# Where the second modulation's rows are stored and fetched, and when the gate's sums are turned

## Chip, cores and metric

The kernel runs on one core of a Trainium2 chip. The metric is the device time of one execution in microseconds, as the median of several runs. The engines named are TensorE (PE, with its weight loads as PEld), VectorE (DVE), ScalarE (ACT), GpSimd (POOL) and SyncE (SP), whose queue issues nearly all DMA transfers here.

## The reference, cut to what matters

A two-layer decoder on 512 tokens of width 2048, in float32. Layer 0 is differential attention; from its output shared keys and values are made, and layer 1 is forgetting attention over them. Each layer has a modulation from a conditioning vector `c`: a shift, a scale and a gate.

```python
c_act = jax.nn.silu(c)
for l in range(DEPTH):
    mod = c_act @ w_mod[l] + b_mod[l]
    shift, scale, gate = jnp.split(mod, 3, axis=-1)
    h = x * (1.0 + scale[:, None]) + shift[:, None]
    if l < N_A:
        y = diff_attention(h, ...)
    else:
        if kv is None:
            kv = shared_kv(x, c_act, kv_w_mod, kv_b_mod, kv_w, kv_b_f)
        y = forgetting_attention(h, b_w_in[l - N_A], b_w_out[l - N_A], *kv)
    x = layer_norm(DN_ALPHA * x + gate[:, None] * y, ln_g[l], ln_b[l])
```

The change is about `mod` of layer 1. Its shift and scale are needed before the first query projection, `h @ w_q`; its gate only at the end.

## The kernel before

**Products.** Every large product is made of float32 numbers split in a high and a low part, so that three matmuls (lines 345 to 347) make one. Weights come as 512 KB steps into staging buffers (`wst`, four of them), ScalarE rounds them to the high part (`whi`, line 245), and VectorE takes the low part (`wlo`, line 246). `WeightStream` (line 176) does this ahead of use: `get` (line 274) sees to it that two further steps are split and up to three further ones loaded. Its loads pass through a hook, `ws.keep`, which is normally the identity.

**Runs, bursts and ticks.** A projection to 512 columns is one call of `group` (line 494), a *run*: 8 steps of two column blocks of the input, each step with four *bursts* of six matmuls, one burst for each of four accumulators. After every burst comes a *tick* (line 478): it takes one entry from the list `pieces` and calls what is in it, and then takes as many steps of the current `background` generator as the run's `bg` says for this tick. Ticks of a run are counted from 0 to 31. So `pieces` and `bg` say beside which burst other work is written down.

**What sets the order.** Outside the kernel's first stage a planner orders each engine's instructions. It goes by the order in which the program writes them down, by when it reckons that data and buffers are there, and so it may put a later instruction first where the earlier one would wait. `tc.keep_in_program_order(ins)` pins an instruction behind the one that was written down last for the same engine. A buffer that is taken again waits until the last use of its former content is over.

**The second modulation.** `w_mod[1]` is not multiplied on TensorE. VectorE scales each 128-row block by its entries of `c_act` and adds it to an accumulator (`macc`). `mod_stream` (line 545) does this for shift and scale, four times 1024 columns with 16 sums each, one sum to a step of the generator; then two steps *turn* the accumulator (transposition and reduction, lines 646 and 647). Five empty steps later a small product on TensorE (line 657) adds up the partial sums. Two additions (line 660) put the bias and the 1 on, and the rows are stored to `mod_dram` (line 661). The steps are spent in the two middle runs of layer 0's output projection (13 ticks each, line 1473), in the first key run (10, line 1947) and in the later key runs (`TICKS`, line 48: 16, 16, and the first nine of the last run).

`end_of_sums` (line 1567) takes all steps that are left. `fetch_rows(1)` (line 1581) reads the rows back in another layout, and `fold(1)` (line 1585) transposes them on TensorE (line 1588) and makes the columns `mod_a` and `mod_b`. From these `build_h` (line 1664) makes the operands of the query projections, 16 blocks of high and low parts, after the steps 3 to 7 of the last key run and directly behind it. It uses two buffers with the tag `htmp`.

**The gate.** The first 1024 columns of the gate begin in the last key run: `gate_start` (line 1489) makes six of 16 sums (`FORE`) with three load buffers (`ms`), and turns them with `turn_gate` (line 1483), also through `htmp`. The first query run goes on with the other ten, in `gate_stream` (line 1516): loads and accumulator are in the buffer `gs` (line 1978). Then come one step for each of two turns, two empty steps, and one step with the product (lines 1547 and 1548), an addition (line 1549) that writes into `gs`, and the store to `gate_dram` (line 1550). `gs` has the same tag as `pT` (line 1983), the turned probabilities of the forgetting attention, and there is one buffer with that tag.

**Query runs.** The runs over `bj[p]` (line 2171) project the queries and gates of two heads each. From `p = 1` on they carry the attention of the pair before in `pieces` (line 2130). Entry 6 of the first pair takes the buffer of `pT` and sends the first block of turned probabilities there (line 2078), entries 16 and 17 multiply by the values (line 2099).

Of the kernel before, what the change touches and what calls it, by code (L numbers as in the profile page):

```python
# [16 lines left out]
P = 128  # L17
D = 2048
KT = D // P
# [29 lines left out]
UNIT = 9  # L49
FORE = 6  # L50
# [3 lines left out]
class Job:  # L54
# [14 lines left out]
    def load(self, nc, dst, s, keep):  # L69
        rows = self.src[2 * s * P : (2 * s + 2) * P, :]  # L70
        off = 0
        for c, n in self.parts:
            keep(nc.sync.dma_start(dst[:, :, off : off + n], rows[:, c : c + n].rearrange("(k p) n -> p k n", p=P)))
            off += n
# [205 lines left out]
def tile_yoco(  # L280
# [23 lines left out]
    nc = tc.nc  # L304
# [19 lines left out]
    mod_dram = [dram.tile([2, D], F32, name=f"mod_dram{k}") for k in range(2)]  # L324
# [8 lines left out]
    def tr_bank(name="tr"):  # L333
        return ps.tile([P, 512], F32, name=name, tag="tr", bufs=1)
# [61 lines left out]
    rows = {}  # L396
# [42 lines left out]
    ws = WeightStream(nc, wpool)  # L439
# [12 lines left out]
    bj = [Job(b_w_in, [(256 * p, 256), (2048 + 256 * p, 256)]) for p in range(8)]  # L452
# [22 lines left out]
    pieces = []  # L475
# [65 lines left out]
    def cols(name):  # L541
        return const.tile([P, KT], F32, name=name)


    def mod_stream(segs, new_stage, new_acc, ahead):

        todo = [(i, kt) for i in range(len(segs)) for kt in range(KT)]
        loaded, turned_sums = [], []

        def load_upto(k):  # L550
            while len(loaded) < min(k + 1, len(todo)):
                i, kt = todo[len(loaded)]
                src, col, _ = segs[i]
                loaded.append(new_stage())
                nc.sync.dma_start(loaded[-1], src[kt * P : (kt + 1) * P, col : col + 1024])

        for k, (i, kt) in enumerate(todo):
            load_upto(min(k + ahead, max([k, *limit[-1:]])) if limit else k + ahead)
            w, one = loaded[k], cact[:, kt : kt + 1]
            loaded[k] = None  # L560
            if kt == 0:
                acc = new_acc()
                ins = V.tensor_scalar(acc, w, one, None, op0=ALU.mult)
            else:
                ins = V.scalar_tensor_tensor(acc, w, one, acc, op0=ALU.mult, op1=ALU.add)  # L565
            tc.keep_in_program_order(ins)
            if kt == 4:
                while turned_sums:
                    next(turned_sums.pop(0), None)
            yield  # L570
            if kt == KT - 1:
                for half, steps in enumerate(segs[i][2]):
                    turned_sums.append(steps(acc[:, 512 * half : 512 * half + 512]))
                    next(turned_sums[-1])
                    yield
        for _ in range(5):
            yield
        for steps in turned_sums:
            next(steps, None)
# [90 lines left out]
    with tc.tile_pool(name="start", bufs=2, reuse_waits="tile") as sp, tc.manual_schedule(engines=MANUAL):  # L670
# [4 lines left out]
        tiles = []  # L675
# [308 lines left out]
        at = [0] * 4  # L984
# [267 lines left out]
    def drain():  # L1252
        while pieces:
            tick(0)
# [9 lines left out]
    def keep(key, acc):  # L1264
        raw[key] = kpool.tile([P, T], F32, name="raw", tag="K")
        S.copy(raw[key], acc)
# [105 lines left out]
    def ktile(name):  # L1372
        return kpool.tile([P, T], F32, name=name, tag="K")
# [105 lines left out]
    ab, rows = {}, {}  # L1479
# [3 lines left out]
    def turn_gate(t, acc, red, f):  # L1483
        V.transpose(t, acc[:, 512 * f : 512 * f + 512])
        V.tensor_reduce(
            red[:, 16 * f : 16 * f + 16], t.rearrange("p (j q) -> p j q", q=32), axis=mybir.AxisListType.X, op=ALU.add
        )

    def gate_start(red, upto):

        tiles = []

        def load():
            tiles.append(npool.tile([P, 1056], F32, name="ms", tag="ms", bufs=3)[:, 0:1024])
            kt = len(tiles) - 1
            nc.sync.dma_start(tiles[kt], w_mod[1][kt * P : (kt + 1) * P, 2 * D : 2 * D + 1024])

        load()
        load()
        yield  # L1500
        acc = npool.tile([P, 2, 512], F32, name="macc", tag="macc", bufs=1).rearrange("p a b -> p (a b)")
        for kt in range(upto):
            if kt + 2 < upto:
                load()
            w, one = tiles[kt], cact[:, kt : kt + 1]
            if kt == 0:
                ins = V.tensor_scalar(acc, w, one, None, op0=ALU.mult)
            else:
                ins = V.scalar_tensor_tensor(acc, w, one, acc, op0=ALU.mult, op1=ALU.add)
            tc.keep_in_program_order(ins)  # L1510
            yield
        for f in range(2):
            turn_gate(npool.tile([P, 512], F32, name="mturn", tag="htmp", bufs=2), acc, red, f)
            yield
# [52 lines left out]
    def end_of_sums():  # L1567
        for _ in background:
            pass
# [8 lines left out]
        return fn  # L1578


    def fetch_rows(k):
        rows[k] = ktile("mrow")
        nc.sync.dma_start(rows[k][0 : 2 * KT, 0:P], mod_dram[k].rearrange("v (a p) -> (v a) p", p=P))

    def fold(k):
        row = rows[k]
        pt = tr_bank()
        PE.transpose(pt[:, 0 : 2 * KT], row[0 : 2 * KT, 0:P], ident[0 : 2 * KT, 0 : 2 * KT])
        a1, b1 = cols(f"mod_a{k}"), cols(f"mod_b{k}")
        V.tensor_tensor(b1, pt[:, KT : 2 * KT], bncol, op=ALU.mult)  # L1590
        V.tensor_tensor(b1, pt[:, 0:KT], b1, op=ALU.add)
        V.tensor_tensor(a1, pt[:, KT : 2 * KT], gcol, op=ALU.mult)
        return a1, b1
# [91 lines left out]
    def evac_k(g):  # L1685
        def fn(b, acc):
            KTs[4 * g + b] = ktile("kT")
            S.copy(KTs[4 * g + b], acc)
        return fn
# [11 lines left out]
    def back_k():  # L1701
        for b in range(TB):
            KTs[b] = ktile("kT")
            nc.sync.dma_start(KTs[b], k_dram[b])
# [208 lines left out]
    for i, (half, s) in enumerate(lag):  # L1913
# [14 lines left out]
        for b in (2 * half, 2 * half + 1):  # L1928
            bs = slice(b * P, (b + 1) * P)
            for kq in range(2):  # L1930
                kt = 2 * s + kq
# [24 lines left out]
    for g in range(1, 4):  # L1956
        if g == 3:
            back_k()
            early = gate_start(gate_first, FORE)
            plan = [None] * 3 + [partial(next, early, None)] * (FORE + 3)  # L1960
            plan += [None] * (UNIT + 7 - len(plan))
            for at, fn in ((UNIT, lambda: (end_of_sums(), fetch_rows(1))), (UNIT + 6, lambda: ab.update(b=fold(1)))):
                plan[at] = [plan[at], fn] if plan[at] else fn
            pieces.extend(plan)
        group(
            kj[g], False, evac_k(g), bg=lambda k, g=g: TICKS[g](k),
            after_sub=(lambda s: build_h(late.get(s, ()), ab.get("b"))) if g == 3 else None,
        )
# [18 lines left out]
    def evac_b(p):  # L1987
        def fn(b, acc):
            hd = 2 * p + b % 2
            if b < 2:  # L1990
                hi = bp.tile([P, T], F32R, name="qh", tag="qh", bufs=2)
                lo = bp.tile([P, T], F32R, name="ql", tag="ql", bufs=2)
                S.activation(hi, acc, AF.Copy, scale=QS)
                V.scalar_tensor_tensor(lo, acc, QS, hi.bitcast(F32), op0=ALU.mult, op1=ALU.subtract)
                cur[hd, "q"] = (hi, lo)
            else:
                th = bp.tile([P, T], F32, name="thb", tag="biasb", bufs=2)
                sg = bp.tile([P, T], F32, name="sgb", tag="sgb", bufs=2)
                S.activation(th, acc, AF.Tanh, scale=0.5)
                V.scalar_tensor_tensor(sg, th, 1.0, acc, op0=ALU.add, op1=ALU.mult)  # L2000
                cur[hd, "sgT"] = sg
        return fn
# [10 lines left out]
    def load_pair(p):  # L2013
        load_v(2 * p)
        for hd in (2 * p, 2 * p + 1):
            nf = bp.tile([P, T], F32, name="nfb", tag="nfb", bufs=2)
            row_bcast(nf, f_dram[hd, :])
            cur[hd, "nf"] = nf
# [131 lines left out]
    def split_ogb(hds):  # L2150
        for hd in hds:
            new_h(hd)
            split(Hh[hd], Hl[hd], ogB[hd])

    load_pair(0)
    for p in range(8):
        if p:
            pieces.extend(attention_pair(p - 1))

        def before(s, p=p):  # L2160
            if s == 7:
                drain()
                if p:
                    load_pair(p)
                split_pair(p)

        def after(s):
            if s >= 1:
                split_ogb((2 * s - 2, 2 * s - 1))

        group(
            bj[p], False, evac_b(p), bg=0 if p > 1 else (lambda k: k < 4 or k == 9) if p else (lambda k: k % 3 == 1),
            before_sub=before, after_sub=after if p == 7 else None,
        )

# [174 lines left out]
```

## Time and profile before

| | us |
|---|---|
| median of 3 runs | 1911.6 |
| lowest and highest run | 1910.22, 1914.89 |
| profiled execution | 1911.24 |
| its span, first to last instruction | 1909.4 |
| mean clock granted to TensorE | 0.999 of full |
| DMA transfers | 402.23 MB |

Times of single instructions below are microseconds from the start of the span. A row of the order in time gives the start, the duration, the engine, the line, the operation with its tiles, and in brackets how long the engine was idle before it and what ended that. TensorE starts a matmul every 0.23 us though a row shows some 0.39, since matmuls overlap. "SPq" rows are issues on SyncE's queue, with the time of issuing. Several issues that follow each other are merged in one row, with the waits between them.

### The profile page before, as it was taken

To read this page: it belongs to the slowest core of one execution; us is meant where nothing else is said; L and a number is where in the kernel's file an instruction comes from. 1 tells how busy PE (TensorE), PEld (TensorE's weight loads), DVE (VectorE), ACT (ScalarE), POOL (GpSimd) and SP (SyncE) were. 2 spreads that over 40 slices of the span, in tenths; PEclk is the share of its full clock that TensorE was granted. 3 is DMA by queue.
4 is the path that set the end of the run, shared out by engine and by line. 5 is a ranking of instruction groups with operands and counts; after the bars stand their busy time and mean duration, and the time that the engine had idled before them with its cause. 6 is when DMAs were issued, how large, how long until landed. Compare 5 with 4: busy or idle time off the path is not lost.

```text
span 1909.4 us, 25683 instructions
## 1 busy us (share of the span) xinstructions
PE 1893.7 (99%) x8829; PEld 1579.2 (83%) x8829; DVE 1433.2 (75%) x2685; ACT 778.6 (41%) x1328; POOL 2.3 (0%) x12
## 2 busy tenths in 40 slices
PE   8999999999999999999999999999999999999998
PEld 7888888888888888888888889887888888888887
DVE  8994588777777778667687877877766666687888
ACT  3656344323333344531275643226344434453122
POOL 0000000000000000000000000000000000000000
PEclk9999999999999999999999999999999999999999
DMA  9993566676767676476658679884655555555952
GB/s 349 385 338 92 155 191 198 213 231 194 235 192 239 190 236 182 133 251 229 189 187 276 211 211 305 304 294 150 203 157 154 151 156 153 160 171 160 323 168 111
DMA packets 350994, 402.23 MB, mean 211 GB/s; under 512 B 77144, under 2 KB 258548, under 8 KB 349584
## 3 DMA queue, kind: packets, MB, share of 16 engines
q1 hardware_dynamic: 347184, 395.20, 65.2%
q10 hardware_dynamic: 3680, 5.40, 0.8%
q8 instruction: 69, 1.13, 0.2%
q14 instruction: 61, 0.50, 0.1%
HBM read 363.46 MB, written 37.04 MB: 210 GB/s over the span
## 4 chain that ended last, share of the span: by engine, by line
PE 92%; DVE 3%; DMA 2%; SPq 1%; issue 1%; ACT 0%; DVEq 0%; ACTq 0%
PE acc L345 24%; PE acc L346 24%; PE acc L347 24%; PE acc L903 4%; PE sc L903 2%; PE sc L347 2%; PE sc L346 2%; PE sc L345 2%; PE o L347 1%; PE o L345 1%; PE o L346 1%; PE o L903 1%; DMA ms<-in_w_mod_dram 1%; SPq L751 1%; DVE wlo L246 0%
## 5 line engine op out<-in xcount | busy, mean ns | idle before, releaser
L245 ACT CAST whi<-wst 128x1024 fp32r<-128x1024 f32 (+2 forms) x294 | 305.4, 1039 | 558.5 <-PE acc L347 217.2
L246 DVE TENSOR_TENSOR wlo<-wst,whi 128x1024 fp32r<-128x1024 f32 (+2 forms) x294 | 354.6, 1206 | 202.4 <-ACT whi L245 192.5
L345 PE MATMUL acc<-hh,whi 128*128 128x512 f32 x1184 | 463.3, 391 | 0.0
L346 PE MATMUL acc<-hl,whi 128*128 128x512 f32 x1184 | 461.5, 390 | 0.0
L347 PE MATMUL acc<-hh,wlo 128*128 128x512 f32 x1184 | 460.6, 389 | 0.0
L345 PE MATMUL acc<-whi,hh 128*128 128x512 f32 (+1 forms) x912 | 353.5, 388 | 0.0
L346 PE MATMUL acc<-wlo,hh 128*128 128x512 f32 (+1 forms) x912 | 352.2, 386 | 0.0
L347 PE MATMUL acc<-whi,hl 128*128 128x512 f32 (+1 forms) x912 | 351.8, 386 | 0.0
L347 PEld LDWEIGHTS acc<-hh,wlo 128*128 128x128 f32 x1184 | 222.3, 188 | 47.3
L345 PEld LDWEIGHTS acc<-hh,whi 128*128 128x128 f32 x1184 | 222.4, 188 | 43.3 <-issue 0.9
L346 PEld LDWEIGHTS acc<-hl,whi 128*128 128x128 f32 x1184 | 222.6, 188 | 42.4
L347 PEld LDWEIGHTS acc<-whi,hl 128*128 128x128 f32 x912 | 171.2, 188 | 35.0 <-DVE hl L1624 0.2
L345 PEld LDWEIGHTS acc<-whi,hh 128*128 128x128 f32 x912 | 171.3, 188 | 32.9 <-ACT hh L1623 0.2
L346 PEld LDWEIGHTS acc<-wlo,hh 128*128 128x128 f32 x912 | 171.4, 188 | 32.4
L618 DVE SCALAR_TENSOR_TENSOR macc<-ms,cact,macc 128x512 f32<-128x512 f32 x180 | 133.7, 743 | 20.8 <-DMA ms<-in_kv_w_mod_dram 13.6
L801 DVE SCALAR_TENSOR_TENSOR sacc<-sms,cact,sacc 128x512 f32<-128x512 f32 (+1 forms) x128 | 89.9, 702 | 5.1 <-DMA sms<-in_w_mod_dram 1.6
L1097 ACT ACTIVATE e<-e,mn 128x128 f32<-128x128 f32 (+3 forms) x64 | 36.1, 563 | 112.1 <-DVE mn L1093 105.5
L565 DVE SCALAR_TENSOR_TENSOR macc<-ms,cact,macc 128x1024 f32<-128x1024 f32 x60 | 76.7, 1278 | 3.2 <-DMA ms<-in_w_mod_dram 2.6
L2057 ACT ACTIVATE eb<-eb,mnb 128x128 f32<-128x128 f32 (+1 forms) x64 | 36.0, 562 | 62.2 <-DVE mnb L2054 62.0
L903 PE MATMUL acc<-wlo,hh 128*128 128x512 f32 x128 | 50.0, 399 | 0.3 <-DVE wlo L265 0.3
L903 PE MATMUL acc<-whi,hl 128*128 128x512 f32 x128 | 49.4, 393 | 0.0
L903 PE MATMUL acc<-whi,hh 128*128 128x512 f32 x128 | 49.2, 393 | 0.0
(414 smaller groups left out, 2511.1 us busy)
## 6 DMA issues: line engine op xcount, KB each, us to landing
wst<-in_a_w_in_dram SPq DMA_DIRECT2D x240, 256.0 KB
ms<-in_w_mod_dram SPq DMA_DIRECT2D x102, 512.0 KB
ms<-in_kv_w_mod_dram SPq DMA_DIRECT2D x64, 512.0 KB
wst<-in_b_w_in_dram SPq DMA_DIRECT2D x128, 256.0 KB
wst<-in_kv_w_dram SPq DMA_DIRECT2D x59, 512.0 KB
sms<-in_w_mod_dram SPq DMA_DIRECT2D x56, 512.0 KB
wst<-in_a_w_out_dram SPq DMA_DIRECT2D x32, 512.0 KB
wst<-in_b_w_out_dram SPq DMA_DIRECT2D x32, 512.0 KB
```

Of the source, the lines that this page charges most:

```text
L245: self.nc.scalar.copy(hi, st)
L246: self.nc.vector.tensor_tensor(lo, st, hi.bitcast(F32), op=ALU.subtract)
L345: PE.matmul(dst, lhs[0], rhs[0], start=start, stop=False, skip_group_check=True)
L346: PE.matmul(dst, lhs[0], rhs[1], start=False, stop=False, skip_group_check=True)
L347: PE.matmul(dst, lhs[1], rhs[0], start=False, stop=stop, skip_group_check=True)
L565: ins = V.scalar_tensor_tensor(acc, w, one, acc, op0=ALU.mult, op1=ALU.add)
L618: ins = V.scalar_tensor_tensor(acc, w, cact[:, kt : kt + 1], acc, op0=ALU.mult, op1=ALU.add)
L751: (queue or nc.sync).dma_start(mtile[n][:, kq : kq + step, v, :], rows.rearrange("(k p) n -> p k n", p=P))
L801: V.scalar_tensor_tensor(acc, w, sc, acc, op0=ALU.mult, op1=ALU.add)
L903: PE.matmul(bank[n, bk], l, r, start=start, stop=stop, skip_group_check=True)
L1097: S.activation(e[:, :w], e[:, :w], AF.Exp, bias=mn, scale=-1.0, accum_out=rs)
L2057: S.activation(e[:, :w], e[:, :w], AF.Exp, bias=mn, scale=-1.0, accum_out=rs)
```

## The change

The last key run gets a new list of pieces. The entries, by tick, before:

| tick | before | after |
|---|---|---|
| 3 | loads for gate sums 1 and 2 | |
| 4 | gate sum 1 | loads for gate sums 1 to 3 |
| 5 | 2 | |
| 6 | 3 | 1 |
| 7 | 4 | 2 |
| 8 | 5 | 3; end of the row sums; fetch of the rows |
| 9 | 6; end of the row sums; fetch of the rows | loads for gate sums 4 to 6 |
| 10, 11 | turns of the gate's two halves | |
| 12, 13, 14 | | 4, 5, 6 |
| 15 | fold of the rows | fold of the rows; turn of the first half |
| 16 | | turn of the second half |

From the fetch to the fold the hook `ws.keep` pins the weight loads, and the fetch itself is pinned. `mod_stream` has three empty steps ahead of its product in place of five. In the first query run the background goes on at ticks 0, 3, ... 27 in place of 1, 4, ... 31, ten steps in place of eleven; in the second at ticks 1, 2, 4, 5 and 11 in place of 0 to 3 and 9.

```diff
@@ mod_stream
-        for _ in range(5):
+        for _ in range(3):
             yield
@@ gate_start
-        load()
-        load()
+        for _ in range(3):
+            load()
         yield
...
         for kt in range(upto):
-            if kt + 2 < upto:
-                load()
+            if kt == 3:
+                while len(tiles) < upto:
+                    load()
+                yield
@@ fetch_rows
-    def fetch_rows(k):
+    def fetch_rows(k, keep=lambda ins: ins):
         rows[k] = ktile("mrow")
-        nc.sync.dma_start(rows[k][0 : 2 * KT, 0:P], mod_dram[k].rearrange("v (a p) -> (v a) p", p=P))
+        keep(nc.sync.dma_start(rows[k][0 : 2 * KT, 0:P], mod_dram[k].rearrange("v (a p) -> (v a) p", p=P)))
@@ last key run
             early = gate_start(gate_first, FORE)
-            plan = [None] * 3 + [partial(next, early, None)] * (FORE + 3)
-            plan += [None] * (UNIT + 7 - len(plan))
-            for at, fn in ((UNIT, lambda: (end_of_sums(), fetch_rows(1))), (UNIT + 6, lambda: ab.update(b=fold(1)))):
-                plan[at] = [plan[at], fn] if plan[at] else fn
-            pieces.extend(plan)
+            go = partial(next, early, None)
+
+            def fetch():
+                end_of_sums()
+                ws.keep = tc.keep_in_program_order
+                fetch_rows(1, ws.keep)
+
+            def turn_rows():
+                ab["b"] = fold(1)
+                ws.keep = lambda ins: ins
+
+            pieces.extend([None] * 4 + [go, None, go, go, [go, fetch], go, None, None, go, go, go, [turn_rows, go], go])
@@ query runs
-            bj[p], False, evac_b(p), bg=0 if p > 1 else (lambda k: k < 4 or k == 9) if p else (lambda k: k % 3 == 1),
+            bj[p], False, evac_b(p), bg=0 if p > 1 else (lambda k: k in (1, 2, 4, 5, 11)) if p else (lambda k: k % 3 == 0 and k < 29),
```

## The prediction

> **What bounds the kernel now.** I read the page's first part, then the busy time by stages, then who waits for whom on TensorE. All rows are of the profile before. The first two are the page's, the next six the windows by stage (columns: stage, its length, then PE, PEld, DVE, ACT, POOL busy with instruction counts, clock, DMA share, GB/s), the last the longest wait of TensorE inside the kernel.
>
> ```profile
> span 1909.4 us, 25683 instructions
> PE 1893.7 (99%) x8829; PEld 1579.2 (83%) x8829; DVE 1433.2 (75%) x2685; ACT 778.6 (41%) x1328; POOL 2.3 (0%) x12
> ```
>
> ```profile
> 0.00:40.00 40.00, 32.95 (x150) 27.34 (x151) 30.95 (x58) 13.87 (x24) 1.66 (x10) 1.00 1.04 342
> ...
> 300.00:800.00 500.00, 499.91 (x2317) 417.20 (x2316) 376.73 (x815) 188.56 (x355) 0.00 (x0) 1.00 0.68 208
> 800.00:990.00 190.00, 189.66 (x871) 156.68 (x870) 132.84 (x245) 63.52 (x102) 0.00 (x0) 1.00 0.65 212
> ...
> 1262.00:1315.00 53.00, 50.70 (x226) 41.70 (x225) 42.31 (x62) 29.34 (x47) 0.00 (x0) 1.00 0.60 201
> ...
> 1358.00:1402.00 44.00, 43.92 (x204) 36.32 (x204) 31.55 (x76) 16.76 (x34) 0.00 (x0) 1.00 0.48 137
> ...
> 1780.00:1909.40 129.40, 123.59 (x545) 101.45 (x544) 108.05 (x159) 29.11 (x39) 0.00 (x0) 0.99 0.55 183
> ```
>
> ```profile
> PE tr L1588 <- DMA mrow<-mod_dram: 2.3, 1, 2.3
> ```
>
> TensorE is the bound nearly everywhere. Its idle time is 1909.4 - 1893.7 = 15.7 us, and the stages shown hold all of it: 7.05 us at the start, 0.09 and 0.34 in the middle, 2.30 in the last key run, 0.08 in the second query run, 5.81 at the end. The change touches neither start nor end, so what it can win is about the 2.30 us. They are one wait: the transposition of the second modulation's rows (line 1588) waits for their fetch.
>
> Now the neighbourhood of that wait: TensorE in order of time, then the chain of work that ended last.
>
> ```profile
> 1281.41 0.31 PE L657 MATMUL tr<-fours,mred 128*128 128x32 f32 x2
> ...
> 1288.22 0.39 PE L347 MATMUL acc<-hh,wlo 128*128 128x512 f32 x1
> ...
> 1289.58 0.39 PE L347 MATMUL acc<-hh,wlo 128*128 128x512 f32 x1
> 1292.26 0.21 PE L1588 MATMUL tr<-ident,mrow 32*128 32x32 f32 x1 [2.29 <-DMA mrow<-mod_dram]
> ```
>
> ```profile
> 1280.83 6.00 DMA ms<-in_w_mod_dram
> ...
> 1288.12 1.23 DVE wlo L246
> ...
> 1289.36 0.37 SPq L73
> ...
> 1289.83 2.30 DMA mrow<-mod_dram
> ```
>
> Read backwards: the rows took 2.30 us to come; their fetch stood on SyncE's queue behind a query weight load (L73); that waited for a stage buffer that a weight split (L246) freed; and the split stood on VectorE behind a gate sum that waited for its own 512 KB load, 6.00 us under way. None of these has to stand ahead of the fetch. TensorE reaches the transposition at 1292.26 - 2.29 = 1289.97, and one burst (six matmuls, 1288.22 to 1289.58) takes 1.36 us.
>
> **The change, part by part.** First the rows' way, on VectorE, on SyncE's queue, and in one stage of the windows.
>
> ```profile
> 1274.01 1.24 DVE L647 TENSOR_REDUCE mred<-mturn 128x16 f32<-128x512 f32 x2
> ...
> 1277.08 1.28 DVE L1509 SCALAR_TENSOR_TENSOR macc<-ms,cact,macc 128x1024 f32<-128x1024 f32 x1
> ...
> 1283.05 0.17 DVE L660 SCALAR_TENSOR_TENSOR mrow<-tr,mrow 64x32 f32<-64x32 f32 x1
> ...
> 1284.58 0.20 DVE L660 SCALAR_TENSOR_TENSOR mrow<-tr,mrow 64x32 f32<-64x32 f32 x1
> ```
>
> ```profile
> 1284.80 0.34 SPq L661 DMA_DIRECT2D mod_dram<-mrow  x1
> 1285.19 4.54 SPq L73 DMA_DIRECT2D wst<-in_b_w_in_dram  x2
> 1289.83 0.41 SPq L1583 DMA_DIRECT2D mrow<-mod_dram  x1
> ...
> 1364.62 0.33 SPq L1550 DMA_DIRECT2D gate_dram<-gs  x1
> ...
> 1367.86 3.71 SPq L2078 DMA_DIRECT2D pT<-turned  x8
> ```
>
> ```profile
> 1288.00:1290.00 2.00, 1.97 (x9) 1.31 (x7) 2.00 (x4) 0.22 (x1) 0.00 (x0) 1.00 0.05 17
> ```
>
> *The product of the row sums (L657).* The background stream needs 4 x 18 = 72 steps to its last turn; 68 are spent before the last key run (13 + 13 + 10 + 16 + 16 ticks), so that turn falls on tick 3. With five empty steps the product is left to the drain at tick 9; with three it comes by itself at tick 7, two bursts earlier: 1281.41 - 2.72 = 1278.69. Its sums are there (the reduction at 1274.01 is over by 1275.25).
>
> *The two additions and the store.* Before, product to store is 3.39 us, since gate sums of 1.28 us stand between and before the additions. After, only the first three sums can. Earliest store: product, 0.31, additions of 0.17 and 0.20, and 0.22 from the last of them to the store (1284.58 to 1284.80): 1279.6. Latest: the same 3.39 us, 1282.1.
>
> *The fetch.* It is now pinned behind the store, and the query loads behind it. It waits for the store to land. No row shows that landing alone; the bounds are the stretch from the later gate store to the first transfer that needed it (1364.62 to 1367.86, 3.24 us) and the moment when all transfers were through (DMA share 0.05 from 1288.0 on). So it is issued between 1282.8 and 1288.0, and with 2.43 us from issue to the transposition's start (1289.83 to 1292.26) the rows are there between 1285.2 and 1290.4. TensorE asks at 1289.97: left over 0 to 0.5 us. I take 0.1, since the early end is the row of the same kind of store. **Term: -2.2 us** (bounds -1.8 and -2.3).
>
> The Trainium skill bears on this place: "DMA: Bandwidth & Descriptors", section "Queues, rings and completion order", says that each DMA engine consumes one queue's descriptors in ring order. By that rule the small store and fetch sit behind the 512 KB gate loads already issued, which is the late end, and the sum would be -1.8 us. The trace agrees in part: the sixth gate load needed 6.00 us.
>
> *What waits behind the pinned fetch.* SyncE holds the query loads (L73) for at most the 5.2 us from 1282.8 to 1288.0. Their tiles are split two steps of four bursts (10.9 us) ahead of use and loaded up to three further steps ahead, so TensorE does not see it: 0, and at most what exceeds that lead.
>
> *Gate sums and gate turns.* Same instructions, other places: three sums of 1.28 us go behind the fetch, and the turns (first two rows below; the third is the stage of that building) go from ticks 10 and 11 to ticks 15 and 16, into the building of the query operands.
>
> ```profile
> 1289.26 1.29 DVE L1484 STREAM_TRANSPOSE mturn<-macc 128x512 f32<-128x512 f32 x2
> 1290.48 1.24 DVE L1485 TENSOR_REDUCE mcol<-mturn 128x16 f32<-128x512 f32 x2
> ```
>
> ```profile
> 1292.30:1315.00 22.70, 22.70 (x101) 18.77 (x102) 19.37 (x37) 20.79 (x37) 0.00 (x0) 1.00 0.31 100
> ```
>
> That adds 2.5 us to a stretch in which VectorE is busy 19.37 of 22.70 us and ScalarE 20.79, and the turns share two buffers (`htmp`) with that building. The operands of the last two of sixteen column blocks would come 2.5 us later, but they are used in the last eighth of the next 43 us run. Cost 0; without that cover 2.5.
>
> *First query run.* Its ten gate sums move one tick forward.
>
> ```profile
> 1328.07 0.75 DVE L1531 TENSOR_SCALAR gs<-gs,cact 128x1024 f32<-128x1024 f32 x1 [5.28 <-DMA gs<-in_w_mod_dram]
> ...
> 1330.59 1.22 DVE L246 TENSOR_TENSOR wlo<-wst,whi 128x1024 fp32r<-128x1024 f32 x1
> ```
>
> A weight split stands behind two sums that wait 5.28 us for data. One more sum ahead of it, or a start 2.5 us later, gives 0 to 3.8 us on VectorE. TensorE is full through that stage; I take 0, and the upper end goes into the range.
>
> *Second query run.* The turns of the gate's sums move to ticks 1 and 2, its product from tick 3 to tick 11, behind this run's sixth score. The buffer `gs`, which the product's addition and store still use, is the one into which the first head's turned probabilities (`pT`) go, and that buffer is taken at tick 6. So its four times four transfers must wait. TensorE, SyncE and VectorE in order of time:
>
> ```profile
> 1364.05 0.23 PE L1548 MATMUL tr<-fours,gred 128*32 128x32 f32 x2
> ...
> 1376.95 0.28 PE L347 MATMUL sc<-kb,ql 128*128 128x256 f32 x1
> ...
> 1387.63 0.40 PE L345 MATMUL o<-pT,vbh 128*128 128x512 f32 x1
> 1389.03 0.50 PE L346 MATMUL o<-pT,vbh 128*128 128x512 f32 x1
> ```
>
> ```profile
> 1378.35 3.06 SPq L2078 DMA_DIRECT2D pT<-turned  x4
> ```
>
> ```profile
> 1388.33 0.65 DVE L2085 TENSOR_TENSOR pT<-pT 128x512 fp32r<-128x512 f32 x1
> ```
>
> Product to first transfer took 3.81 us (1364.05 to 1367.86). After, the product comes at 1377.2 (the score, 1376.95, and 0.28), so the first transfer at 1381.0. Sixteen at 3.71 / 8 = 0.46 us each end at 1388.4; before, the last ended at 1381.41. The split of the last block followed 6.92 us behind that and took 0.65. Taking as little as 2.30 us of transfer and two passes of 0.65, or as much as before, it ends between 1392.0 and 1396.0 instead of 1388.98: **3.0 to 7.0 us late** for the second value product. What TensorE loses hangs on the order the planner writes: a burst takes 1.36 us, so two to five bursts pulled ahead of the values hide it all; with the old order it is 3.0 to 7.0 us. The rows at 1387.63 and 1389.03 show which is nearer: between the first value product and the second, which needs the split, stands just about one burst. The planner fills such waits with bursts. I take 0 and keep 7.0 for the range.
>
> *The sum.* -2.2 + 0 + 0 + 0 + 0 = -2.2 us. The profiled execution took 1911.24 us (span 1909.4); it would be 1909.0. The median of the runs, 1911.6, lies 0.4 above it, so I forecast 1909.4. A measurement of this kernel tells about 0.3% (5.7 us) from no change; this is 0.12%.
>
> **The rivals.**
>
> *Rows late.* The sixth gate load may stay ahead of the store on SyncE's queue and the rows come behind it, at 1290.4 or a little after. For it speak the 6.00 us of that load, against it that all transfers were through by 1288.0. Then -1.5 to -1.8: about 1910.0.
>
> *The change doesn't do what it says.* The pins hold on SyncE only behind what was issued before, and the planner can still hoist the later gate loads, whose buffers come free early, past the store. If the fetch is then as late as it was: 1911.6. Against it speaks that the query load it stood behind (1285.19, 4.54 us) is pinned after it now.
>
> *Slower: the turned probabilities late.* In the second query run the values of the first head stand at their old place on TensorE while the `pT` transfers wait for the gate store. The price is 3.0 to 7.0 us as worked out, against 2.2 won, so it is slower from a wait over 2.2 us on, and ends at 1912.4 to 1916.4; with a wait as long for the second head up to 1923. For it speaks that tick 11 comes after tick 6, certain in the code; against it the filling just described, and that the stage before was 43.92 of 44.00 us full with transfers just as tight. "TensorE: Matmul & The Clock Gate", section "Part 1: The HAM clock gate", of the Trainium skill states that an idle window of some 3.4 us halves TensorE's clock until as much busy time has passed; by that page a wait of 7.0 us would cost an estimated 1.7 us more. The trace has no such wait inside the kernel: after the 2.29 us its clock reads 1.00.
>
> *Faster by more* has no place: all idle time between 40 and 1780 us is 2.81 us.
>
> **How the numbers follow.** Forecast 0.65; rows late 0.11; no effect 0.07; slower through late probabilities 0.14; a split late in the first query run or a reordering elsewhere 0.03. The low end is the full 2.3 us below the lowest run of before (1910.22), 1907.9; the high end takes in no effect and the rival's lower half, 1914.0. What lies outside is the rival's upper half, 0.07, and scatter. Faster by over 0.3%: 0.02, for a reordering at the kernel's end. Slower by over 0.3%: 0.05, the rival with both heads or with a late split. Within: 0.93.
>
> **What would show it.** Right: the wait of line 1588 gone from TensorE's waits, the fetch issued before 1288 and ahead of all query loads, the product near 1278.7, the last key run's stage full. In the second query run the product near 1377 and the first `pT` transfer near 1381 (both less 2.3 us), with value products some bursts later and no gap. Wrong: a wait of TensorE or its weight loads at the values (lines 345 to 347, `pT`), at a weight split, or a remaining wait at line 1588 of over 0.5 us; or a first `pT` transfer that is not late at all, which would refute my reading of the buffer.

## The result, and the profile after

| | before | after |
|---|---|---|
| median, us | 1911.9 | 1909.12 |
| lowest and highest run, us | 1909.9, 1915.54 | 1907.14, 1912.98 |
| runs | 22 | 22 |
| profiled execution, us | 1911.24 | 1910.16 |
| its span, us | 1909.4 | 1908.3 |

The ratio is 0.9984 (95% interval 0.9977 to 0.999): 3.1 us less, between 1.9 and 4.4 (the two medians differ by 2.8). That is within 0.3%, and the median lies 0.3 us below the forecast of 1909.4. But the sum hides three things: the rows won a little more than forecast, the change made a new wait, and the later query runs became shorter, which no step of the prediction had.

First the page of the changed kernel (its span, then busy time by engine), then its windows; the columns are those of the windows of before: length, then busy time of TensorE, weight loads, VectorE, ScalarE, GpSimd, then granted clock, DMA share and GB/s.

```profile
span 1908.3 us, 25694 instructions
...
PE 1893.2 (99%) x8829; PEld 1580.0 (83%) x8829; DVE 1433.6 (75%) x2685; ACT 778.3 (41%) x1328; POOL 2.3 (0%) x12
```

```profile
1262.00:1315.00 53.00, 53.00 (x236) 43.60 (x235) 41.74 (x61) 28.68 (x45) 0.00 (x0) 1.00 0.60 204
1315.00:1358.00 43.00, 41.25 (x183) 33.85 (x182) 28.45 (x31) 14.77 (x20) 0.00 (x0) 1.00 0.72 233
1358.00:1402.00 44.00, 44.00 (x204) 36.48 (x205) 30.74 (x73) 16.45 (x33) 0.00 (x0) 1.00 0.48 144
```

The last key run, which was 2.30 us short of full, is full. The next stage, the first query run, now has 43.00 - 41.25 = 1.75 us idle; before it had none:

```profile
1315.00:1358.00 43.00, 43.00 (x191) 35.63 (x190) 27.61 (x28) 15.01 (x19) 0.00 (x0) 1.00 0.76 251
```

TensorE's waits of the changed kernel name it (time, number, longest):

```profile
PE acc L345 <- DVE ql L2003: 1.7, 1, 1.7
```

So a wait of 2.29 us went and one of 1.75 us came 65 us later. The rows' way, SyncE's queue of the changed kernel in order of time:

```profile
1279.85 0.33 SPq L661 DMA_DIRECT2D mod_dram<-mrow  x1
1280.26 2.65 SPq L1496 DMA_DIRECT2D ms<-in_w_mod_dram  x2
1283.00 0.39 SPq L1585 DMA_DIRECT2D mrow<-mod_dram  x1
1283.44 37.08 SPq L73 DMA_DIRECT2D wst<-in_b_w_in_dram  x15
```

The fetch is issued 6.8 us earlier than at 1289.83, ahead of every query load. The transposition of the rows, by its tile, with its first and last start, before and after:

```profile
L1588 PE MATMUL tr<-ident,mrow x2: 215/229/243, 832.8 to 1292.3; 32*128 32x32 f32 x2
```

```profile
L1590 PE MATMUL tr<-ident,mrow x2: 243/246/248, 833.4 to 1290.3; 32*128 32x32 f32 x2
```

From the first layer's transposition to the second's it was 459.5 us and is 456.9. Such a stretch between two fixed events is the better measure here, since the time at which the kernel reaches 832 differs from execution to execution by up to 2 us (832.3 to 834.3 in the traces below).

Two more marks split the rest: ScalarE's first copy of a query (`qh`) in the second query run and in the last one. Before, then after:

```profile
1403.90 0.60 ACT L1993 ACTIVATE qh<-acc 128x512 fp32r<-128x512 f32 x1 [0.54 <-PE acc L347]
...
1710.84 0.60 ACT L1993 ACTIVATE qh<-acc 128x512 fp32r<-128x512 f32 x1 [0.48 <-PE acc L347]
```

```profile
1403.85 0.60 ACT L2002 ACTIVATE qh<-acc 128x512 fp32r<-128x512 f32 x1 [0.34 <-PE acc L347]
...
1709.86 0.60 ACT L2002 ACTIVATE qh<-acc 128x512 fp32r<-128x512 f32 x1 [0.48 <-PE acc L347]
```

The three stretches, in us, from the same rows of each profiled kernel, with the ratio to before (interval). The kernels are those of the next section; the first query stretch runs from the rows' transposition to the second run's copy, the later ones from there to the last run's.

| kernel | rows to rows | first query stretch | later query runs | ratio |
|---|---|---|---|---|
| before | 459.49 | 111.64 | 306.94 | |
| after | 456.93 | 113.56 | 306.01 | 0.9984 (0.9977 to 0.999) |
| e1 after again | 457.02 | 112.69 | 306.39 | 0.998 (0.9971 to 0.9989) |
| e2 rows only | 457.04 | 114.09 | 306.97 | 0.9995 (0.9986 to 1.0003) |
| e3 ticks only | 459.68 | 111.49 | 306.38 | 0.9993 (0.9984 to 1.0002) |
| e4 after, split pinned | 456.94 | 111.72 | 306.02 | 0.9981 (0.9972 to 0.999) |
| e5 rows only, split pinned | 457.09 | 111.69 | 306.96 | 0.9986 (0.9978 to 0.9995) |
| e6 early product | 456.93 | 111.67 | 306.94 | 0.9988 (0.9979 to 0.9997) |
| e7 turns first | 456.94 | 111.52 | 306.10 | 0.9983 (0.9974 to 0.9992) |
| e8 gate product at tick 15 | 456.95 | 112.17 | 310.96 | 1.0007 (0.9999 to 1.0016) |
| e9 early product and ticks | 456.91 | 111.55 | 306.17 | 0.9986 (0.9977 to 0.9995) |
| e10 late product | 457.14 | 111.59 | 306.03 | 0.9987 (0.9978 to 0.9995) |

By it the change is -2.56 for the rows, +1.92 for the first query stretch, -0.93 for the later runs.

### The profile page after: what moved, and what is told of

It reads as the page before. It is cut to its first block, busy times and chain, and to the rows that moved or that the text cites. A ratio compares the mean times of both kernels' runs of the same rounds, so it can differ in the third digit from the quotient of the medians.

```text
span 1908.3 us, 25694 instructions
## 1 busy us (share of the span) xinstructions
PE 1893.2 (99%) x8829; PEld 1580.0 (83%) x8829; DVE 1433.6 (75%) x2685; ACT 778.3 (41%) x1328; POOL 2.3 (0%) x12
## 4 chain that ended last, share of the span: by engine, by line
PE 94%; DVE 3%; DMA 1%; SPq 1%; issue 0%; ACT 0%; DVEq 0%; ACTq 0%
PE acc L345 25%; PE acc L346 25%; PE acc L347 25%; PE acc L903 4%; PE sc L903 2%; PE sc L347 2%; PE sc L346 2%; PE sc L345 2%; PE o L347 1%; PE o L345 1%; PE o L346 1%; PE o L903 1%; SPq L751 1%; DMA sms<-in_w_mod_dram 0%; DMA vld<-v_dram 0%
```

## The experiments

**e1 to e4: which part does what.** The changed kernel unchanged (e1); the change without the new ticks of the gate stream in the query runs (e2); those ticks alone, put into the kernel before (e3); and the changed kernel with one pin (e4). The theory was that the new wait starts at ScalarE. Its row and VectorE's, at the end of the first query run of the changed kernel:

```profile
1354.34 0.62 ACT L340 CAST vbh<-vld 128x512 fp32r<-128x512 f32 x1 [8.28 <-DMA vld<-v_dram]
1354.87 1.04 ACT L245 CAST whi<-wst 128x1024 fp32r<-128x1024 f32 x1
```

```profile
1355.94 1.23 DVE L246 TENSOR_TENSOR wlo<-wst,whi 128x1024 fp32r<-128x1024 f32 x1 [1.97 <-ACT whi L245]
1357.09 0.69 DVE L2003 SCALAR_TENSOR_TENSOR ql<-acc,qh 128x512 fp32r<-128x512 f32 x1
```

On ScalarE the copy of the second head's values (`vbh`) stands ahead of a copy of query weights (`whi`) and waits 8.28 us for the values' load; behind `whi` come VectorE's half of the split (`wlo`) and of the query (`ql`), and TensorE waits for that query, since the bank that holds it is needed next. In the kernel before the same copy stood at the same place:

```profile
1351.06 0.62 ACT L340 CAST vbh<-vld 128x512 fp32r<-128x512 f32 x1 [3.10 <-DMA vld<-v_dram]
```

e2 and e3 differ from the changed kernel and from the one before by the ticks alone:

```diff
@@ e2: after, with the old ticks
-            bj[p], False, evac_b(p), bg=0 if p > 1 else (lambda k: k in (1, 2, 4, 5, 11)) if p else (lambda k: k % 3 == 0 and k < 29),
+            bj[p], False, evac_b(p), bg=0 if p > 1 else (lambda k: k < 4 or k == 9) if p else (lambda k: k % 3 == 1),
@@ e3: before, with the new ticks
-            bj[p], False, evac_b(p), bg=0 if p > 1 else (lambda k: k < 4 or k == 9) if p else (lambda k: k % 3 == 1),
+            bj[p], False, evac_b(p), bg=0 if p > 1 else (lambda k: k in (1, 2, 4, 5, 11)) if p else (lambda k: k % 3 == 0 and k < 29),
@@ e4: after, with the second head's copy of values behind what stands ahead of it in the text
-    def split_v(hd):
+    def split_v(hd, keep=None):
...
+        if keep:
+            keep(S.copy(vh[:, :, es], cur[hd, "vld"]))
+            V.tensor_tensor(vl[:, :, es], cur[hd, "vld"], vh[:, :, es].bitcast(F32), op=ALU.subtract)
+            return
...
-        later_v, split_later = partial(load_v, 2 * p + 1), partial(split_v, 2 * p + 1)
+        later_v, split_later = partial(load_v, 2 * p + 1), partial(split_v, 2 * p + 1, tc.keep_in_program_order if p == 0 else None)
```

e1:

> The changed kernel once more. Theory: the 2.3 us wait for the rows is gone in every execution, and the 1.7 us wait at the end of the first query run (a split of values on ScalarE that waits for its load) comes only in some, since the medians differ by 2.8 us and the two profiled executions by 1.1. So: ratio 0.9980 to 0.9990, no wait at the rows' transposition, and a wait of 0 to 1 us at the accumulator in the first query run. Rival: that wait is part of the changed kernel; then it is 1.5 to 2 us again, and the median's 2.8 us must come from a place outside the profiled span or elsewhere in it.

e2:

> The changed kernel with the query runs' ticks as before (1, 4, ... 31 and 0 to 3, 9). Theory: the gain is the rows' alone and the late turned probabilities cost nothing: ratio as of the changed kernel, 0.9980 to 0.9990, first transfer of turned probabilities within 3 us of the tick-6 score again (some 9 us after the run's start), no wait at the values. Rival, late probabilities cost: 1.5 us or more faster than the changed kernel (ratio below 0.9976). Rival, the moved ticks bring part of the gain: 0.9990 or above.

e3:

> The kernel before with only the query runs' ticks changed. Theory: 0.9997 to 1.0003; the wait for the rows stays at 2.3 us, the first transfer of turned probabilities moves from 1367.9 to about 1381, the value products some 6 to 9 us later, and TensorE has no wait there. Rival, late probabilities cost: 1.001 or more, with a wait at the values or behind them. Rival, the ticks bring part of the gain: 0.9995 or less.

e4:

> The changed kernel with ScalarE's split of the second head's values (first pair only) pinned to its written place, tick 8 of the second query run, so that the weight rounding no longer stands behind it. Theory: no wait at the accumulator at the end of the first query run in any execution; ratio to the kernel before 0.9975 to 0.9988, up to 0.9 us (0.0005) below the changed kernel if the wait comes in half of the executions. Rival, the wait has another cause (late weights): it stays at 1 to 2 us.

Measured medians: before 1912.88, e1 1909.54, e2 1912.33, e3 1910.46, e4 1908.6. The expectations of e2 and e3 were missed: their ratios, 0.9995 and 0.9993, lie where the rival put them by which the ticks bring part of the gain, though neither interval excludes no change. The table of stretches separates the kernels better than the ratios do. The rows' edit wins its 2.5 us with the old ticks too (e2) and loses about as much again in the first query stretch, in two waits of 0.7 us shown there (for `ql`, then for `sgb`) and what goes with them. The ticks alone (e3) keep the old wait and shorten the later runs by 0.56. The pin (e4) takes the new wait away and keeps the rest. The new wait was 0.8 us in e1, the same kernel as after: its size differs between executions.

**e5: is the blocked copy all of the loss?** e2 with the pin of e4.

> Rows edit alone (old places of the gate stream in the query runs) with ScalarE's split of the second head's values kept in its place. Theory (the rows win 2.5 us at the fold; all that was lost in the first query run is ScalarE waiting for the values' load ahead of a weight split): from the rows' fold to the first query's copy 111.7 us instead of 114.1, no wait at ql or sgb, the later query runs as slow as before (306.9 from the first query's copy to that of the last run), so 2.4 us under before: ratio 0.9987. Rival (the loss hangs on the gate stream's old places too): a wait at ql or sgb stays, 113 to 114 us, ratio 0.9995.

1909.51 against 1912.45, 0.9986. The first query stretch is 111.69, as before, and the later runs 306.96. So the loss does not hang on the ticks, and the copy of the values accounts for all of it, both waits of e2 included.

**e7: why did the values come late?** The gate's turns moved into the building of the query operands (the products of `htmp`). Its last instruction is an `hl`. VectorE and SyncE, before, then after:

```profile
1317.84 0.69 DVE L341 TENSOR_TENSOR hl<-htmp,hh 128x512 fp32r<-128x512 f32 x1
```

```profile
1319.89 1.60 SPq L1523 DMA_DIRECT2D gs<-in_w_mod_dram  x3
...
1346.88 0.43 SPq L2006 DMA_DIRECT2D vld<-v_dram  x1
```

```profile
1320.04 0.68 DVE L341 TENSOR_TENSOR hl<-htmp,hh 128x512 fp32r<-128x512 f32 x1
```

```profile
1322.82 9.27 SPq L1525 DMA_DIRECT2D gs<-in_w_mod_dram  x5
...
1346.84 0.42 SPq L2015 DMA_DIRECT2D vld<-v_dram  x1
```

The gate's 512 KB loads start only when the building is over, 1.4 us behind it before and 2.1 after, and the load of the second head's values is issued behind the last of them. Since the transposition comes 2 us earlier, the same 1346.8 is 1.9 us later as counted from it (56.55 against 54.62). e7 puts the turns ahead of the building, and the last three gate sums one tick earlier to make room for them:

```diff
-            pieces.extend([None] * 4 + [go, None, go, go, [go, fetch], go, None, None, go, go, go, [turn_rows, go], go])
+            pieces.extend([None] * 4 + [go, None, go, go, [go, fetch], go, None, go, go, go, go, [go, turn_rows]])
```

> The changed kernel with gate sums 4 to 6 at ticks 11 to 13, both turns at ticks 14 and 15 and thus ahead of the building of the query operands instead of inside it. Theory (the turns inside the building make it end 2.2 us later, the gate loads of the first query run start 3 us later, and the second head's values land behind them): the last hl at about 1318, gate loads from about 1320, no wait at ql, fold to first query's copy 111.7; 1 to 2 us under the changed kernel, ratio to before 0.998. The fold itself may be late by up to 0.7 us, since the turns stand ahead of it. Rival (the loss comes from the rows' earlier fold or from the order alone, not from the turns): building ends early and the wait at ql of 0.8 to 1.7 us stays, 112.7 to 113.6.

1908.54, 0.9983; the first query stretch 111.52, no wait at `ql`. The rows lost nothing by it (456.94). Counted from the transposition, the last `hl` ends at 27.9 us (before 26.3, after 30.4) and the first gate load is issued at 29.2 (before 27.6, after 32.5). The theory holds. The kernels without the pin of e4 and e5 side by side, in us from the rows' transposition; the last column is the first wait of TensorE that is shown there:

| kernel | first gate load | values' load issued | their copy starts | TensorE waits |
|---|---|---|---|---|
| e3 | 27.7 | 53.4 | 57.9 | 0 |
| e9 | 27.8 | 54.0 | 58.4 | 0 |
| e6 | 28.8 | 54.5 | 58.7 | 0 |
| before | 27.6 | 54.6 | 58.8 | 0 |
| e7 | 29.2 | 54.7 | 60.3 | 0 |
| e10 | 32.6 | 56.4 | 62.0 | 0 |
| e2 | 32.4 | 57.5 | 63.0 | 0.7 |
| e1 | 32.2 | 57.2 | 63.1 | 0.8 |
| after | 32.5 | 56.6 | 64.1 | 1.7 |
| e8 | 32.6 | 57.8 | 64.7 | 2.4 |

Beyond some 62.3 us each microsecond of the copy is one of waiting. With the turns inside the building the values' load is issued 1.7 to 3.1 us later than in e7. The rest is the transfer itself, 4.2 us from issue to copy before, 5.5 in e7 and 5.5 to 7.5 in the kernels below it. That the fuller queue makes it longer was not tried by itself.

**e6, e9, e10: what brought the rows early?** e6 changes the kernel before in two numbers: three empty steps ahead of the product, fetch one tick earlier. No new places for the gate loads, no pins. e9 adds the new ticks. e10 is the changed kernel with the five empty steps again.

```diff
@@ e6 and e9: before
-        for _ in range(5):
+        for _ in range(3):
...
-            for at, fn in ((UNIT, lambda: (end_of_sums(), fetch_rows(1))), (UNIT + 6, lambda: ab.update(b=fold(1)))):
+            for at, fn in ((UNIT - 1, lambda: (end_of_sums(), fetch_rows(1))), (UNIT + 6, lambda: ab.update(b=fold(1)))):
@@ e10: after
-        for _ in range(3):
+        for _ in range(5):
```

> Before, with three empty steps instead of five ahead of the product and the fetch one tick earlier; gate loads, turns and query runs as before. By the planner's order four gate loads stand ahead of the store and one query load between store and fetch. Theory (the product's place is nearly all, the loads ahead cost a few tenths; the building starts earlier by as much and the turns stand ahead of it, so no delay of the first query run): the wait at the rows' transposition 0 to 0.7 us, fold to fold 457.0 to 457.7, fold to first query's copy 111.6; 1.8 to 2.5 us under before, ratio 0.9987 to 0.9991. Rival (my steps on record: the loads ahead of the store and the query load ahead of the fetch keep the rows late, so the fixed places are what counts): a wait of 1 us or more stays, ratio 0.9995 or more.

> The small edit of the rows (three empty steps instead of five, fetch one tick earlier) with the changed kernel's ticks of the gate stream in the query runs; gate loads and turns at their old places. Theory: fold to fold 456.9 (the product's place alone), fold to first query's copy 111.6 (turns ahead of the building), from there to the last run's 306.1 (no query run in which the first product of a head's values starts within 0.1 us of ScalarE's copy, 50.99 us each): 2.5 and 0.9 less than before, 3.4 in all, ratio 0.9982. Rival (the two parts don't add, since the smaller distance of the gate stream's start brings the wait at a query split back): 113 us to the first query's copy, ratio 0.999.

> The changed kernel with five empty steps ahead of the product again: fixed places, loads and ticks of the change, the product two ticks later. Theory (the product's place is what brought the rows early, the fixed places nothing): by the planner's order two query loads stand between store and fetch again, the wait at the rows' transposition is 2 us or more, fold to fold 459.0 to 459.7; the turns are still inside the building, the ticks still win 0.9; in all 0.5 under to 1 over before, ratio 0.9997 to 1.0005. Rival (my steps on record: the fixed places keep the queue free for the store and the fetch, and win most of the 2.2 without the earlier product): fold to fold under 458, a wait under 1 us, ratio 0.9985 to 0.999.

e6 1909.65 (0.9988), e9 1908.59 (0.9986), e10 1909.45 (0.9987; before 1911.78 for e9 and e10, 1912.45 for e6). e6 and e9 came out as the theory had it, in the stretches that it named. **e10 refutes it**: with the late product the rows still come in time. SyncE's queue of e6, then of e10:

```profile
1280.69 0.38 SPq L661 DMA_DIRECT2D mod_dram<-mrow  x1
...
1286.56 0.34 SPq L1583 DMA_DIRECT2D mrow<-mod_dram  x1
```

```profile
1283.65 0.38 SPq L661 DMA_DIRECT2D mod_dram<-mrow  x1
1284.13 0.90 SPq L73 DMA_DIRECT2D wst<-in_b_w_in_dram  x2
1287.76 0.34 SPq L1585 DMA_DIRECT2D mrow<-mod_dram  x1
```

Counted from the first layer's transposition, the fetch was issued at 457.06 before, and at 449.64 after, 454.19 in e6, 453.26 in e9, 453.97 in e10; TensorE asks at about 456.9, and the rows need 2.4 us. It had to come 2.6 us earlier; the whole change brought 7.4. Either half brings enough without the other: the product two ticks earlier (e6, e9), or three gate sums written down behind the fetch (e10). In e10 all six gate loads still stand ahead of the store and two query loads between store and fetch, but these are issued within 0.90 us, where before they took 4.54. The fetch stands one tick earlier in e6, e9 and e10 alike (e10's product, too, comes 1.3 us earlier than that of before, counted from the first transposition), and that step alone was not run. Nor were the pins by themselves; e6 and e9 get their rows in time without any.

That e10 has 457.14 where e6 has 456.93 is not the rows' doing: its transposition follows the matmul before it at the same 0.3 us as in the changed kernel, and TensorE's wait for ScalarE at 981 us (a score of the stage before) is 0.44 us there instead of 0.22.

**e8: where does the slower rival begin?** The gate's product of the second query run four ticks later still.

```diff
-            bj[p], False, evac_b(p), bg=0 if p > 1 else (lambda k: k in (1, 2, 4, 5, 11)) if p else (lambda k: k % 3 == 0 and k < 29),
+            bj[p], False, evac_b(p), bg=0 if p > 1 else (lambda k: k in (1, 2, 4, 5, 15)) if p else (lambda k: k % 3 == 0 and k < 29),
```

> The changed kernel with the gate's product of the second query run at tick 15 instead of 11: by 43.4 / 32 = 1.36 us a tick some 5.4 us later, 1382.8, the first transfer of the first head's turned probabilities at 1386.6, the last at 1394, the last split at 1397.6 to 1401.6. Theory (the planner puts bursts ahead of the values as long as it has some in the run): no wait at the values, the time of the changed kernel (ratio 0.998). Rival (my slower rival: the values come to stand before the split, at the run's end no burst is left): TensorE waits 2 to 6 us at the values, lines 345 to 347 with pT, ratio 0.9995 to 1.0015.

1913.27, 1.0007, some 3.7 us over e1; the two were timed on different occasions, each against before. The theory had the time wrong, the rival the place. The first value product comes at 1403.6, 7 us later than after's, and does not wait. TensorE's waits of e8:

```profile
PE acc L345 <- DVE ql L2003: 2.4, 1, 2.4
PE sc L345 <- DVE mnb L2063: 1.1, 1, 1.1
```

The second is a score of the third query run that waits for VectorE to have read its bank, probably since the late values of the run before have pushed VectorE's work together there. And each later run takes 51.3 us instead of 51.0. That points to why the later runs of the change are shorter. In the kernel before, TensorE and ScalarE around the second head's first value product of a later query run:

```profile
1458.67 0.39 PE L347 MATMUL acc<-hh,wlo 128*128 128x512 f32 x1
1458.90 0.50 PE L345 MATMUL o<-pT,vbh 128*128 128x512 f32 x1
1459.24 0.40 PE L345 MATMUL acc<-hh,whi 128*128 128x512 f32 x1
```

```profile
1458.23 0.61 ACT L2084 CAST pT<-pT 128x512 fp32r<-128x512 f32 x1
```

The same in the changed kernel:

```profile
1509.12 0.40 PE L345 MATMUL o<-pT,vbh 128*128 128x512 f32 x1
1509.35 0.39 PE L345 MATMUL acc<-hh,whi 128*128 128x512 f32 x1
```

```profile
1507.77 0.61 ACT L2093 CAST pT<-pT 128x512 fp32r<-128x512 f32 x1
```

And in e8:

```profile
1513.16 0.39 PE L345 MATMUL acc<-hh,whi 128*128 128x512 f32 x1
1513.40 0.50 PE L345 MATMUL o<-pT,vbh 128*128 128x512 f32 x1
1513.74 0.40 PE L346 MATMUL acc<-hl,whi 128*128 128x512 f32 x1
```

```profile
1512.73 0.61 ACT L2093 CAST pT<-pT 128x512 fp32r<-128x512 f32 x1
```

Before, the product starts 0.06 us behind the end of ScalarE's copy that it needs (1458.23 + 0.61), lasts 0.50 instead of 0.40, and the next matmul starts 0.34 later instead of 0.23. In the changed kernel the copy is over by 1508.38, the product has 0.74 to spare, and the distance is 0.23. The profile shows no wait at the first. From the fourth query run to the seventh there is one such place a run before, in e2, e5 and e6 (51.11 us a run), none in after, e1, e3, e4, e7, e9 and e10 (50.99), and two in e8 (51.30). For those four runs e3 shows that the new ticks did it, e2 that nothing else did. The last run is another matter: it takes 51.37 us up to its copy before and 50.98 in after, but 51.37 again in e1 and e3. The instructions of after and e1 are the same and in the same order, so these 0.39 us come only in some executions (in e1 a value product of that run, line 346, starts 0.28 us later behind the matmul before it than in after). Of the 0.93 us, 0.55 came in every kernel with the new ticks but e8. The edit names none of those runs: their order is the planner's, and it comes out otherwise once the first values stand later. A kernel that moves these products and nothing else was not tried.

## Why the prediction was right, and where it was not

- **Rows.** Right in the mechanism, and at the early end of every bound: product at 1279.08 (forecast 1278.69, with an execution that was 0.6 later), store 1279.85 (1279.6 to 1282.1), fetch 1283.00 (1282.8 to 1288.0), no wait left. The term was -2.2 with a bound of -2.3. At the transposition it was 2.36: from the start of the matmul before it took 2.68 us (1289.58 to 1292.26) and now takes 0.32:

```profile
1289.97 0.39 PE L347 MATMUL acc<-hh,wlo 128*128 128x512 f32 x1
1290.29 0.24 PE L1590 MATMUL tr<-ident,mrow 32*128 32x32 f32 x1
```

  The stretch from rows to rows won 2.4 to 2.6. Most of the rest is TensorE's wait for ScalarE at 980 us, which was 0.35 before and reads 0.19 to 0.44 in the others, the change or not. The rows that come 2.43 us after a fetch at 1283.00 had 4.9 us to spare, and e6 and e10 show that half the change would have done. The planner did hoist gate loads past their written places, as the second rival feared: of the three that are written down behind the fetch, one is issued ahead of the store and two between store and fetch (1280.26), without harm. With all six ahead of the store (e6) the fetch came 5.87 us behind it instead of 3.15, and SyncE waited 4.4 us of that for the store to land; it was still in time, since TensorE does not ask before 456.9. The Trainium skill's rule ("DMA: Bandwidth & Descriptors", section "Queues, rings and completion order"), by which the late end would hold, agrees with that delay in e6; in the changed kernel the early end held.
- **Query loads behind the pinned fetch: 0.** Right.
- **Gate turns in the building of query operands: 0.** This is the step that failed. The prediction looked for the price at the users of the operands, the last eighth of the next run, and there is none there. The gate loads start at the building's end, they stand ahead of the values' load, and ScalarE stands still for the values ahead of a weight split. +1.0 to +1.9 us in two executions of the same kernel; nothing in e7, where the turns stand ahead of the building.
- **First query run: 0, 3.8 on VectorE for the range.** The place was right (a weight split late), the engine was not: the split's first half, on ScalarE, behind the values, not VectorE's half behind a gate sum. "TensorE is full through that stage" was no cover: a full engine shows that it didn't wait before, not how near the next wait is. It was 3.5 us away (58.8 to 62.3).
- **Second query run: 0.** Right. Product and first transfer came at the forecast times:

```profile
1376.94 0.23 PE L1550 MATMUL tr<-fours,gred 128*32 128x32 f32 x2
...
1396.44 0.51 PE L345 MATMUL o<-pT,vbh 128*128 128x512 f32 x1
1397.95 0.40 PE L346 MATMUL o<-pT,vbh 128*128 128x512 f32 x1
```

```profile
1381.07 7.76 SPq L2087 DMA_DIRECT2D pT<-turned  x16
```

  The second value product is 8.9 us later than at 1389.03 (forecast 3.0 to 7.0), and the planner put bursts ahead of it, as the prediction supposed. e8 adds another 7 us without a wait there. So the slower rival, which priced 2.2 us of lateness as enough to lose, did not come true: no wait stood at the values at all. The Trainium skill's rule of "TensorE: Matmul & The Clock Gate", section "Part 1: The HAM clock gate", stays without a test: the longest wait of TensorE shown between 40 and 1780 us was 2.6 us (e3, for the rows), and the clock of the changed kernel's three stages reads 1.00.
- **"Faster by more has no place".** Wrong in kind: the idle time that the windows show is not all that can be won. Four query runs at 0.12 us make about 0.5 us, in a kernel whose windows had nothing left to win there; the 0.4 in the last run of after is no fixed part of the change, since e1 lacks it.
- **The sum.** -2.2 was forecast. The parts make -2.56 + 1.92 - 0.93 - 0.13 (the end, after the last run's copy) = -1.7 for the profiled execution and -2.1 for that of e1, while the runs give -3.1 (1.9 to 4.4). That the forecast came so close is in part luck: a loss of 1.0 to 1.9 us and a gain of 0.5 to 0.9, neither of them foreseen, nearly cancel. The interval reaches down to the parts, and two profiled executions of one kernel alone differ by 0.9 in the new wait; whether 1 us more lies elsewhere stays open.

e4, e7, e9 and e10 have neither of the two waits and the shorter later runs. Their medians (1908.6, 1908.54, 1908.59, 1909.45) lie under e1's 1909.54, but the intervals overlap, and no run tells them apart from each other or from the change. e9 gets there with two numbers and the ticks.

## What to carry to other kernels

When work is moved into a stage on a helper engine, follow not only who uses that stage's results but also which loads start at its end, what is queued behind them, and which engine stands still for the last of them. When an edit wins, take it apart: here either of two halves would have brought the rows in time, and a third part lost half of the win again. And compare stretches between fixed events of the trace: from rows to rows the ten kernels without the old wait lie within 0.25 us, while their medians differ by more. A second execution is needed even so: after and e1 are one kernel, and their later stretches differ by 0.9 and 0.4 us.

## What the runs showed of the hardware

A matmul whose operand comes just in time costs without a wait being shown: 0.34 us to the next start instead of 0.23, and 0.50 us long, when it starts 0.05 us behind ScalarE's end. With 0.28 us to spare it costs nothing: in the changed kernel, at 1459.04, it is 0.40 long and the next starts 0.23 later. A shown wait costs more than its figure: in e8 the matmuls on both sides of the wait of 2.38 start 2.77 us apart, where 0.23 is usual, and the next one starts another 0.33 later:

```profile
1355.43 0.39 PE L347 MATMUL acc<-hh,wlo 128*128 128x512 f32 x1
1358.20 0.50 PE L345 MATMUL acc<-hh,whi 128*128 128x512 f32 x1 [2.38 <-DVE ql L2003]
1358.53 0.39 PE L346 MATMUL acc<-hl,whi 128*128 128x512 f32 x1
```

That is 2.54 + 0.10 = 2.6 us for 2.38 shown. The Trainium skill, "TensorE: Matmul & The Clock Gate", section "Part 2: What happens when you issue a matmul", states that the drain of one matmul is hidden under the fill of the next only while they follow each other closely; the rows agree, with 0.1 us more to the next start; that it is this overlap that is lost was not tried by itself. At the rows the difference was smaller: 2.36 us from start to start for 2.29 shown.
